# Seven-product sums in a transformer MLP: VectorE and ScalarE in written order while they run

## The chip, the cores and the metric

The kernel runs on one core of one Trainium2 chip. The metric is device time in microseconds (us) of one launch. Engines: TensorE (PE: matmuls, PEld: its weight loads), VectorE (DVE), ScalarE (ACT), GpSimd (POOL) and SyncE (SP, which issues the loads). SBUF is the working memory; PSUM holds matmul results in banks of 128 x 512 float32.

## The reference

Two residual layers over 256 positions and 2048 channels in float32. Each ends with a large MLP and a gated embedding; the token mixers ahead of the MLP are not touched by the change.

```python
for i in range(DEPTH):                      # DEPTH = 2
    ...                                     # token mixer, x = x + mixer(x) @ W_out
    h = rms_norm(x, mlp_norm[i])
    x = x + jnp.square(jax.nn.relu(h @ mlp_w1[i])) @ mlp_w2[i]     # 2048 -> 8192 -> 2048
    g = jax.nn.sigmoid(rms_norm(x, ple_norm[i]) @ ple_w_gate[i])
    x = x + g * (p[i] @ ple_w_proj[i])
return rms_norm(x, final_norm)
```

## The kernel before

Every float32 weight is used as two rounded halves, high and low, and every product as three matmuls (high-high, high-low, low-high). A weight tile of 128 x 2048 (1 MB) is loaded by SyncE into one of four raw buffers (`raw`, line 96). ScalarE writes its high half (L112), VectorE the low half as raw minus high (L117), both into one of four buffers `hl`. A matmul that reads the low half therefore waits for VectorE, one that reads only the high half for ScalarE. `Weights.run_ahead` (L129) issues splits up to three tiles ahead of the tile in use and loads two further ahead, unless `ws.hold` sets a lower limit on the splits.

The MLP of a layer runs over eight steps f = 0..7. A step for f < 7 is, in TensorE's order: block `w1(2f+2)` (first MLP matrix, four tiles, PSUM tiles `ps_h`), `w2(f,2)` and `w2(f,3)` (two column blocks of the second matrix, `ps_o`, two tiles each), then `pair(f)`, then block `w1(2f+3)`. Step 7 has no first block; it runs `w2(7,2)`, `pair(7)`, `pair_end`, `w2(7,3)`, and goes on to the embedding (`ps_e`, `ps_g`).

`pair(f)` makes the other two column blocks of the second matrix with seven products in place of eight, for two hidden blocks: fourteen products of six matmuls each, from seven `hl` tiles with two products in each. Numbered 0 to 13 in TensorE's order, the products of the second hidden block are 7 to 13; by their names p they are 1, 5, 2, 6, 3, 7, 4. Some weight operands are sums of raw tiles (VectorE, L109), so one tile here costs VectorE up to two additions and two half splits of 128 x 1024. The results stand in three PSUM pairs of banks, a (products 1 and 5), b (2 and 3), c (7 and 6), and a single bank d (4). `gather` takes them out when they are complete: a and c into `sums` (L657; for f = 0 by ScalarE, L655), b and d into x (L649, L651). There are three pairs of banks (`mm_pool`), so the two PSUM tiles of the next block `w1(2f+3)` take the pairs that a and b leave, and the block after it takes c first. `sm_pool` has two single banks: d and the transposes `tr_ple` share them.

Order: TensorE and SyncE keep the order of the code. For VectorE and ScalarE a list scheduler sets the order by priority, except inside `in_order()` (L255), where they too keep the order of the code; line 710 raises the priority of `pair_end` and line 751 on belongs to the embedding. `put_off` and `tick` delay a piece of code by so many steps; one product of the pair is a step, and so is one fourth of a tile elsewhere. `after.chunk(c, steps)` (L330) takes squares of a block of x on ScalarE and, `steps` later, transposes it on TensorE and writes it as `xT_ple` halves (L275, L280).

Of the kernel before, what the change touches and what calls it, by code (L numbers as in the profile page):

```python
# [29 lines left out]
PRIO = 400  # L30
# [119 lines left out]
def encoder(ctx: ExitStack, tc: tile.TileContext, a, out: bass.AP):  # L150
# [11 lines left out]
    ws = Weights(nc, raw_pool, hl_pool, 3, 2)  # L162
# [92 lines left out]
    def in_order():  # L255
        return tc.manual_schedule(engines={mybir.EngineType.Activation, mybir.EngineType.DVE})
# [5 lines left out]
    def tick():  # L262
        for entry in later[:]:
            entry[0] -= 1
            if entry[0] <= 0:
                later.remove(entry)
                entry[1]()
# [76 lines left out]
    def psum_mm(name):  # L344
        return mm_pool.tile([P, 1024], F32, tag="mm", name=name)
# [223 lines left out]
    def mlp(i, norm, after):  # L569
# [58 lines left out]
        def w2(f, n):  # L628
            ps = psum_mm(f"ps_o{i}_{f}_{n}")
            for q in (2 * f, 2 * f + 1):  # L630
                rows_product(ps, hidden[q], range(4), q == 2 * f, q == 2 * f + 1)
            add_to_x(ps, n)

        def pair(f):


            tiles = {}

            def psum(p):

                key, half = {1: ("a", 0), 5: ("a", 1), 2: ("b", 0), 3: ("b", 1), 7: ("c", 0), 6: ("c", 1), 4: ("d", 0)}[p]
                if key not in tiles:
                    name = f"ps_s{i}_{f}{key}"
                    tiles[key] = sm_pool.tile([P, 512], F32, tag="sm", name=name) if key == "d" else psum_mm(name)
                return tiles[key][:, half * 512:(half + 1) * 512]

            def gather(p):
                if p == 3:
                    nc.vector.tensor_tensor(x[:, 0, :1024], tiles["b"], x[:, 0, :1024], ALU.add)  # L649
                elif p == 4:  # L650
                    nc.vector.tensor_tensor(x[:, 1, :512], tiles["d"], x[:, 1, :512], ALU.add)  # L651
                elif p in (5, 7):
                    ps, to = (tiles["a"], sums[:, :1024]) if p == 5 else (tiles["c"], sums[:, 1024:])
                    if f == 0:
                        nc.scalar.activation(to, ps, AF.Copy)  # L655
                    else:
                        nc.vector.tensor_tensor(to, ps, to, ALU.add)  # L657

            k = 0
            for q in (2 * f, 2 * f + 1):  # L660
                h, g = hidden[q], forms[q]
                for p in SEVEN[q % 2]:
                    if k % 2 == 0:
                        w = ws.next()
                    for kt in range(2):
                        for m, (s, j) in enumerate(PASSES_W_MOVES):
                            act = {1: h[:, s, kt, :P], 2: h[:, s, 2 + kt, :P], 4: h[:, s, 2 + kt, P:], 5: g[:, s, 0, kt],
                                   6: g[:, s, 1, kt], 7: g[:, s, 2, kt], 3: g[:, s, 3, kt]}[p]
                            col = (k % 2) * 1024 + kt * 512
                            nc.tensor.matmul(psum(p), lhsT=act, rhs=w[:, j, col:col + 512],  # L670
                                             start=q % 2 == 0 and kt == 0 and m == 0,
                                             stop=q % 2 == 1 and kt == 1 and m == 2)
                    tick()
                    k += 1
                    if q % 2 and p in (6, 7, 4):
                        for done in {6: (5,), 7: (3,), 4: (7, 4)}[p]:
                            gather(done)

        def pair_end():
            m1, m5, m7, m6 = (sums[:, k * 512:(k + 1) * 512] for k in range(4))  # L680
            c11, c12, c21, c22 = (x[:, t, n * 512:(n + 1) * 512] for t in range(2) for n in range(2))
            add, sub = ((lambda to, p, q, op=op: nc.vector.tensor_tensor(to, p, q, op)) for op in (ALU.add, ALU.subtract))
            add(c11, c11, m1)
            sub(m6, m6, m1)
            sub(c21, c21, m6)
            add(c21, c21, m7)
            after.chunk(0, 10)
            sub(m5, m6, m5)
            add(c12, c12, m5)
            add(c22, c22, m5)  # L690
            sub(c22, c22, m7)
            after.chunk(1, 13)
# [5 lines left out]
        for f in range(8):  # L698
            if f < 7:
                w1(2 * f + 2)  # L700
            w2(f, 2)
            if f < 7:
                w2(f, 3)
                pair(f)
                w1(2 * f + 3)
                continue
            pT = embedding(i)
            after.chunk(2)
            pair(f)
            with tc.high_priority(offset=PRIO):  # L710
                pair_end()
            w2(f, 3)
            after.chunk(3, 8)
        return pT

    def embedding(i):
        pt = work.tile([P, 2, S], F32, name="pt", tag="sv")
        nc.sync.dma_start(out=pt, in_=a["pT"][i])
        pT = act_pool.tile([P, 2, 2, S], F32R, tag="act", name=f"pT{i}")
        divide_psum(halves(pT), pt, None)  # L720
        return pT
# [51 lines left out]

    nple = Norm("ple0", R_PLE)
    pT = mlp(0, norm, nple)
    norm = Norm("od", R_OD)
    order = ctx.enter_context(ExitStack())
# [70 lines left out]

    nple = Norm("ple1", R_PLE + 16)
    pT = mlp(1, norm, nple)  # L850
    gfin = act_pool.tile([P, D], F32, tag="act", name="gfin")
    nc.scalar.dma_start(out=gfin, in_=a["final_norm"].partition_broadcast(P))
# [110 lines left out]
```

## Time and profile before

| | |
|---|---|
| median of 3 runs | 2024.72 us (2023.49 to 2027.61) |
| profiled execution | 2022.2 us, span 2020.4 us |
| TensorE busy | 1947.5 us, 96% of the span |
| VectorE busy | 1564.6 us, 77% |
| ScalarE busy | 1043.6 us, 52% |
| granted TensorE clock, mean | 0.993 |
| HBM read | 373.75 MB, 186 GB/s over the span |

A row of the timeline gives the start in us from the span's start, the length, the engine, the line, what is written and read, and how many equal instructions follow each other; in brackets stands the idle time just before and what ended it. TensorE's matmuls overlap, so the length of a group is a little more than the distance to the next group's start. VectorE's instructions overlap by about 0.08 us in the same way.

### The profile page before, as it was taken

How to read it: one execution, taken by the hardware profiler on the slowest of the kernel's cores; microseconds unless marked ns; L12 is line 12 of the kernel's file. 1: busy time of each engine (PE TensorE's matmuls, PEld its weight loads, DVE VectorE, ACT ScalarE, POOL GpSimd, SP SyncE). 2: the span in 40 equal slices, each digit the busy share in tenths (PEclk: the TensorE clock that was granted, in tenths of full speed). 3: DMA queues.
4: the chain of work that ended last, by engine and by line, in shares of the span. 5: the costliest groups of instructions: out<-in, count | busy, mean ns of one | idle time of the engine just before them, and what ended most of it. 6: DMA issues, size and time to landing. Idle time of an engine off the chain costs nothing.

```text
span 2020.4 us, 24088 instructions
## 1 busy us (share of the span) xinstructions
PE 1947.5 (96%) x9730; PEld 1650.4 (82%) x9730; DVE 1564.6 (77%) x1771; ACT 1043.6 (52%) x1087; POOL 128.8 (6%) x65
## 2 busy tenths in 40 slices
PE   8999999999999999999999999999999999999897
PEld 6888888878787887877789888887887878787686
DVE  7988768796888869689656557977879687788854
ACT  6445555555455545545545445555545455455543
POOL 3875000000000000000001000000000000000000
PEclk9999999999999999999999999999999999999899
DMA  8545553645545464544443545545464554645532
GB/s 336 181 174 208 198 177 146 250 176 200 190 164 215 146 243 163 212 187 162 175 166 125 192 184 187 204 159 220 146 229 157 220 197 156 227 148 193 219 137 103
DMA packets 55664, 377.43 MB, mean 187 GB/s; under 512 B 6384, under 2 KB 6528, under 8 KB 11648
## 3 DMA queue, kind: packets, MB, share of 16 engines
q1 hardware_dynamic: 55152, 374.82, 50.6%
q8 instruction: 76, 1.25, 0.2%
q10 hardware_dynamic: 144, 1.05, 0.2%
q14 instruction: 36, 0.29, 0.0%
q0 software_dynamic: 256, 0.02, 0.0%
HBM read 373.75 MB, written 2.10 MB: 186 GB/s over the span
## 4 chain that ended last, share of the span: by engine, by line
PE 78%; DVE 17%; issue 3%; ACT 1%; DMA 1%; SPq 0%; ACTq 0%; DVEq 0%
PE ps_h L593 22%; PE ps_o L358 16%; PE ps_h L598 12%; DVE hl L117 10%; PE ps_g L358 8%; PE ps_od L358 4%; PE ps_in L358 4%; DVE raw L109 3%; PE ps_out L358 3%; PE ps_pool L358 2%; PE ps_outp L358 1%; PE ps_e L358 1%; DVE x L649 1%; DVE x L379 1%; PE ps_f L371 1%
## 5 line engine op out<-in xcount | busy, mean ns | idle before, releaser
L112 ACT ACTIVATE hl<-raw 128x2048 fp32r<-128x2048 f32 (+2 forms) x529 | 778.3, 1493 | 716.9 <-PE ps_h L598 281.1
L117 DVE TENSOR_TENSOR hl<-raw,hl 128x2048 fp32r<-128x2048 f32 (+3 forms) x501 | 863.2, 1745 | 325.4 <-ACT hl L112 324.0
L593 PE MATMUL ps_h<-xT_mlp,hl 128*128 128x512 f32 x2048 | 493.2, 392 | 28.6 <-DVE x L649 28.6
L593 PEld LDWEIGHTS ps_h<-xT_mlp,hl 128*128 128x128 f32 x2048 | 377.5, 189 | 106.8 <-issue 33.3
L358 PE MATMUL ps_o<-hl,h 128*128 128x512 f32 x1536 | 352.4, 390 | 0.0
L358 PEld LDWEIGHTS ps_o<-hl,h 128*128 128x128 f32 x1536 | 288.1, 188 | 59.3
L598 PEld LDWEIGHTS ps_h<-xT_mlp,hl 128*128 128x128 f32 x2048 | 262.8, 191 | 10.1
L598 PE MATMUL ps_h<-xT_mlp,hl 128*128 128x256 f32 x2048 | 266.1, 283 | 0.0
L358 PE MATMUL ps_g<-hl,xT_ple 128*128 128x512 f32 (+1 forms) x816 | 180.6, 382 | 0.0
L358 PEld LDWEIGHTS ps_g<-hl,xT_ple 128*128 128x128 f32 x816 | 148.1, 191 | 28.6 <-DVE hl L117 0.4
L117 POOL TENSOR_TENSOR hl<-raw,hl 128x2048 fp32r<-128x2048 f32 (+1 forms) x28 | 120.7, 4325 | 55.9 <-ACT hl L112 55.9
L358 PE MATMUL ps_in<-hl,xT_ev 128*128 128x512 f32 x384 | 90.8, 398 | 7.5 <-ACT hl L112 7.5
L455 DVE SCALAR_TENSOR_TENSOR acc<-vp,vT,acc 128x256 f32<-128x256 f32 x240 | 96.4, 485 | 0.1
L358 PEld LDWEIGHTS ps_in<-hl,xT_ev 128*128 128x128 f32 x384 | 73.3, 192 | 23.2 <-ACT hl L112 7.5
L608 ACT ACTIVATE relu<-ps_h 128x512 f32<-128x512 f32 x64 | 38.3, 598 | 97.4 <-PE ps_h L598 97.4
L358 PE MATMUL ps_od<-hl,f 128*128 128x512 f32 x384 | 88.1, 390 | 0.0
L358 PEld LDWEIGHTS ps_od<-hl,f 128*128 128x128 f32 x384 | 71.8, 188 | 14.7
L109 DVE TENSOR_TENSOR raw<-raw 128x1024 f32<-128x1024 f32 x64 | 78.1, 1220 | 0.6
L109 DVE TENSOR_TENSOR raw<-raw,raw 128x1024 f32<-128x1024 f32 x64 | 78.1, 1220 | 0.0
L609 DVE TENSOR_TENSOR relu<-ps_h,relu 128x512 f32<-128x512 f32 x64 | 43.8, 688 | 29.8 <-ACT relu L608 29.8
L812 POOL CAST top<-z 128x4 fp32r<-128x4 f32 x8 | 1.5, 188 | 907.8 <-DVE z L280 907.8
L624 ACT ACTIVATE g<-form 128x512 fp32r<-128x512 f32 x64 | 38.3, 624 | 22.6 <-DVE form L621 11.7
(283 smaller groups left out, 1695.7 us busy)
## 6 DMA issues: line engine op xcount, KB each, us to landing
raw<-in_mlp_w SPq DMA_DIRECT2D x256, 1024.0 KB, 4.9
raw<-in_ple_w_gate SPq DMA_DIRECT2D x32, 1024.0 KB, 4.9
raw<-in_w_in SPq DMA_DIRECT2D x20, 1024.0 KB, 4.8
raw<-in_ev_w_out SPq DMA_DIRECT2D x16, 1024.0 KB, 4.7
raw<-in_od_w_out SPq DMA_DIRECT2D x16, 1024.0 KB, 4.8
raw<-in_w_in SPq DMA_DIRECT2D x16, 256.0 KB, 6.1
raw<-in_ple_w_proj SPq DMA_DIRECT2D x8, 512.0 KB, 3.4
x<-in_x SPq DMA_DIRECT2D x2, 1024.0 KB, 7.8
```

The source lines that it names most:

```text
L109: self.nc.vector.tensor_tensor(src, src, self.raw[other[0]][:, other[1]:other[1] + w], ALU.add)
L112: self.nc.scalar.activation(hl[:, 0, to], src, AF.Copy)
L117: getattr(self.nc, lo).tensor_tensor(hl[:, 1, to], src, hl[:, 0, to].bitcast(F32), ALU.subtract)
L358: nc.tensor.matmul(ps[t][:, cols], lhsT=acts[:, s, kt, t * P:(t + 1) * P], rhs=w[:, m, kt * 512 + cols.start:kt * 512 + cols.stop], start= ...
L371: nc.tensor.matmul(out_ps, lhsT=w[sw], rhs=act[sa], start=bank_first and i == 0, stop=i == n - 1, skip_group_check=True)
L379: nc.vector.tensor_tensor(xs, ps[:, t * 512:(t + 1) * 512], xs, ALU.add)
L455: nc.vector.scalar_tensor_tensor(acc, src, cwT[:, ch, k:k + 1], acc, ALU.mult, ALU.add)
L593: nc.tensor.matmul(pss[p][:, e], lhsT=w[:, 0, ch], rhs=norm.xT[c][:, :, kt], start=c == 0 and kt == 0, stop=False, skip_group_check=True)
L598: nc.tensor.matmul(pss[p][:, e, 1], lhsT=w[:, 1, ch], rhs=norm.xT[c][:, 0, kt], start=False, stop=c == 3 and kt == 3, skip_group_check=True)
L608: nc.scalar.activation(r, pss[p][:, :, 1], AF.Copy)
L609: nc.vector.tensor_tensor(s, pss[p][:, :, 0], r, ALU.add)
L624: nc.scalar.activation(g[:, 0, to], src, AF.Copy)
```

## The change

Three things change. In `pair`, the splits of the tiles behind the pair's own seven are held back until product 3 of the second hidden block (number 11) has been issued; then `ws.hold` gets its old value. The evictions of a and b (`gather` 5 and 3) stand together behind product 3; those of c and d stand together at the end as before. And VectorE and ScalarE keep the order of the code in every pair, in the last one through `pair_end` too, whose raised priority goes. In the last step the transposes of the third block of x move from 4 steps behind the call to 16, which is behind the pair, into `w2(7,3)`.

```diff
@@ pair(f)
+            hold, ws.hold = ws.hold, min(ws.hold, ws.used + 7)
             k = 0
             for q in (2 * f, 2 * f + 1):
...
-                    if q % 2 and p in (6, 7, 4):
-                        for done in {6: (5,), 7: (3,), 4: (7, 4)}[p]:
+                    if q % 2 and p in (3, 4):
+                        for done in {3: (5, 3), 4: (7, 4)}[p]:
                             gather(done)
+                        ws.hold = hold
@@ mlp, steps 0 to 6
-                pair(f)
+                with in_order():
+                    pair(f)
                 w1(2 * f + 3)
@@ mlp, step 7
             pT = embedding(i)
-            after.chunk(2)
-            pair(f)
-            with tc.high_priority(offset=PRIO):
+            after.chunk(2, 16)
+            with in_order():
+                pair(f)
                 pair_end()
             w2(f, 3)
```

VectorE, step 1 of the first layer, from the last addition into raw79 on: hl84 and hl85 are the pair's last two tiles, hl86 to hl88 the first three of the next block, and ps_s0_1a, 1b, 1c, 1d the results a to d. Before:

```order
L117 TENSOR_TENSOR hl84_3445<-raw79_3370,hl84_3445 128x1024
L109 TENSOR_TENSOR raw78_3338<-raw78_3338,raw79_3370 128x1024
L117 TENSOR_TENSOR hl85_3467<-raw79_3370,hl85_3467 128x1024
L117 TENSOR_TENSOR hl84_3445<-raw78_3338,hl84_3445 128x1024
L657 TENSOR_TENSOR sums_119<-ps_s0_1a_3411,sums_119 128x1024
L109 TENSOR_TENSOR raw78_3338<-raw78_3338 128x1024
L117 TENSOR_TENSOR hl86_3488<-raw80_3443,hl86_3488 128x2048
L117 TENSOR_TENSOR hl85_3467<-raw78_3338,hl85_3467 128x1024
L117 TENSOR_TENSOR hl87_3505<-raw81_3465,hl87_3505 128x2048
L117 TENSOR_TENSOR hl88_3523<-raw82_3486,hl88_3523 128x2048
L649 TENSOR_TENSOR x_81<-ps_s0_1b_3418,x_81 128x1024
L657 TENSOR_TENSOR sums_119<-ps_s0_1c_3452,sums_119 128x1024
```

After, from the same place:

```order
L109 TENSOR_TENSOR raw78_3341<-raw78_3341,raw79_3373 128x1024
L117 TENSOR_TENSOR hl84_3450<-raw79_3373,hl84_3450 128x1024
L117 TENSOR_TENSOR hl84_3450<-raw78_3341,hl84_3450 128x1024
L109 TENSOR_TENSOR raw78_3341<-raw78_3341 128x1024
L117 TENSOR_TENSOR hl85_3472<-raw79_3373,hl85_3472 128x1024
L117 TENSOR_TENSOR hl85_3472<-raw78_3341,hl85_3472 128x1024
L657 TENSOR_TENSOR sums_119<-ps_s0_1a_3416,sums_119 128x1024
L649 TENSOR_TENSOR x_81<-ps_s0_1b_3423,x_81 128x1024
L117 TENSOR_TENSOR hl86_3521<-raw80_3448,hl86_3521 128x2048
L117 TENSOR_TENSOR hl87_3526<-raw81_3470,hl87_3526 128x2048
L117 TENSOR_TENSOR hl88_3529<-raw82_3491,hl88_3529 128x2048
L657 TENSOR_TENSOR sums_119<-ps_s0_1c_3457,sums_119 128x1024
```

The pair's own splits now come first, then the evictions of a and b, then the next block's three splits; before, the three splits stood ahead of the eviction of b, one of them ahead of the pair's last split.

VectorE at the end of step 7 of the first layer: hl193 is the pair's last tile, hl194 to hl196 are for `w2(7,3)` and `ps_e`, L682 and L685 are lines of `pair_end`. Before:

```order
L117 TENSOR_TENSOR hl193_6982<-raw168_6825,hl193_6982 128x1024
L657 TENSOR_TENSOR sums_119<-ps_s0_7a_6907,sums_119 128x1024
L117 TENSOR_TENSOR hl196_7038<-raw172_7001,hl196_7038 128x1024
L649 TENSOR_TENSOR x_81<-ps_s0_7b_6914,x_81 128x1024
L657 TENSOR_TENSOR sums_119<-ps_s0_7c_6967,sums_119 128x1024
L682 TENSOR_TENSOR x_81<-x_81,sums_119 128x512
L682 TENSOR_TENSOR sums_119<-sums_119 128x512
L651 TENSOR_TENSOR x_81<-ps_s0_7d_6988,x_81 128x512
```

After:

```order
L117 TENSOR_TENSOR hl193_6986<-raw168_6846,hl193_6986 128x1024
L657 TENSOR_TENSOR sums_119<-ps_s0_7a_6930,sums_119 128x1024
L649 TENSOR_TENSOR x_81<-ps_s0_7b_6937,x_81 128x1024
L117 TENSOR_TENSOR hl194_7035<-raw170_6962,hl194_7035 128x2048
L117 TENSOR_TENSOR hl195_7040<-raw171_6984,hl195_7040 128x2048
L117 TENSOR_TENSOR hl196_7043<-raw172_7005,hl196_7043 128x1024
L657 TENSOR_TENSOR sums_119<-ps_s0_7c_6971,sums_119 128x1024
L651 TENSOR_TENSOR x_81<-ps_s0_7d_6992,x_81 128x512
```

Here hl194 and hl195, which before stood ahead of hl193's last half, stand behind the evictions of a and b and ahead of those of c and d.

## Rows read from the trace of the kernel before

**Rows 1.** The page: span, and busy time of each engine.
```profile
span 2020.4 us, 24088 instructions
PE 1947.5 (96%) x9730; PEld 1650.4 (82%) x9730; DVE 1564.6 (77%) x1771; ACT 1043.6 (52%) x1087; POOL 128.8 (6%) x65
```
**Rows 2.** TensorE's waits: waiting and waited for, us in total, times, longest.
```profile
PE ps_h L593 <- DVE x L649: 28.6, 12, 2.4
PE ps_s_7d L670 <- DVE xT_ple L280: 7.7, 2, 4.4
...
PE ps_s_1d L670 <- DVE hl L117: 1.0, 2, 0.5
```
**Rows 3.** Timeline of TensorE, first layer, steps 0 and 1.
```profile
341.49 1.52 PE L670 MATMUL ps_s_0a<-hl,h 128*128 128x512 f32 x6
...
360.53 3.79 PE L593 MATMUL ps_h<-xT_mlp,hl 128*128 128x512 f32 x16
...
426.82 1.52 PE L670 MATMUL ps_s_1a<-hl,h 128*128 128x512 f32 x6
...
441.78 1.52 PE L670 MATMUL ps_s_1b<-hl,g 128*128 128x512 f32 x6
...
444.50 0.39 PE L670 MATMUL ps_s_1d<-hl,h 128*128 128x512 f32 x1
445.41 1.43 PE L670 MATMUL ps_s_1d<-hl,h 128*128 128x512 f32 x5 [0.51 <-DVE hl L117]
446.67 1.98 PE L593 MATMUL ps_h<-xT_mlp,hl 128*128 128x512 f32 x8
451.04 2.08 PE L593 MATMUL ps_h<-xT_mlp,hl 128*128 128x512 f32 x8 [2.39 <-DVE x L649]
```
**Rows 4.** Timeline of TensorE, first layer, start of the pair of step 2.
```profile
515.62 1.52 PE L670 MATMUL ps_s_2a<-hl,h 128*128 128x512 f32 x6
```
**Rows 5.** Timeline of VectorE, first layer, the pair of step 1.
```profile
427.02 1.29 DVE L379 TENSOR_TENSOR x<-ps_o,x 128x512 f32<-128x512 f32 x2 [0.44 <-PE ps_o L358]
...
430.50 1.22 DVE L109 TENSOR_TENSOR raw<-raw,raw 128x1024 f32<-128x1024 f32 x1
...
441.93 7.82 DVE L117 TENSOR_TENSOR hl<-raw,hl 128x2048 fp32r<-128x2048 f32 x4
...
449.67 1.22 DVE L649 TENSOR_TENSOR x<-ps_s_1b,x 128x1024 f32<-128x1024 f32 x1
450.81 1.22 DVE L657 TENSOR_TENSOR sums<-ps_s_1c,sums 128x1024 f32<-128x1024 f32 x1
```
**Rows 6.** Timeline of ScalarE, first layer, behind the pair of step 1.
```profile
449.14 1.91 ACT L112 ACTIVATE hl<-raw 128x2048 fp32r<-128x2048 f32 x1 [3.76 <-DMA raw<-in_mlp_w]
```
**Rows 7.** Groups by line and shape: count, busy us, mean ns, idle before.
```profile
L117 DVE TENSOR_TENSOR hl<-raw,hl 128x2048 fp32r<-128x2048 f32 x252 | 576.5, 2294 | 310.6 <-ACT hl L112 309.9
...
L117 DVE TENSOR_TENSOR hl<-raw,hl 128x1024 fp32r<-128x1024 f32 x232 | 277.5, 1220 | 9.4 <-ACT hl L112 8.6
...
L112 ACT ACTIVATE hl<-raw 128x1024 fp32r<-128x1024 f32 x236 | 243.3, 1057 | 216.8 <-DVE raw L109 90.3 <-PE ps_o L358 67.6 <-PE ps_g L358 12.2
```
**Rows 8.** The page's DMA issues: count, size, median us to landing.
```profile
raw<-in_mlp_w SPq DMA_DIRECT2D x256, 1024.0 KB, 4.9
```
**Rows 9.** Timeline of TensorE, step 7: first layer, then one row of the second.
```profile
926.42 1.52 PE L670 MATMUL ps_s_7a<-hl,h 128*128 128x512 f32 x6
...
952.79 11.92 PE L358 MATMUL ps_o<-hl,h 128*128 128x512 f32 x48
...
1878.52 2.90 PE L670 MATMUL ps_s_7d<-hl,h 128*128 128x512 f32 x6 [4.40 <-DVE xT_ple L280]
```
**Rows 10.** Timeline of VectorE, step 7: first layer, then one row of the second.
```profile
934.10 1.23 DVE L109 TENSOR_TENSOR raw<-raw,raw 128x1024 f32<-128x1024 f32 x1
...
964.98 1.29 DVE L379 TENSOR_TENSOR x<-ps_o,x 128x512 f32<-128x512 f32 x2
...
1885.00 1.23 DVE L657 TENSOR_TENSOR sums<-ps_s_7a,sums 128x1024 f32<-128x1024 f32 x1 [1.50 <-PE ps_s_7a L670]
```

## The prediction

> **What bounds the kernel now.** I read the page first. TensorE is busy 96% of 2020.4 us, VectorE 77%, ScalarE 52% [rows 1], so time can be won only where TensorE stands still, about 73 us in all. The table of TensorE's waits says where: 28.6 us in 12 waits of at most 2.4 us end with the eviction of b (L649), six lines like the one shown (steps 1 to 6, two layers each) give another 6 us for a low half that VectorE had not written, and 7.7 us in two waits belong to step 7 [rows 2]. Third, the timeline of steps 0 and 1. In step 0 the pair starts at 341.49 and the block behind it runs through from 360.53. In step 1 the last product is cut in two (444.50, then 445.41 after a wait for `hl`), and the block stops after eight matmuls until 451.04, for 2.39 us, on L649 [rows 3]. From pair start to pair start step 0 takes 426.82 - 341.49 = 85.33 us and step 1 takes 515.62 - 426.82 = 88.80 [rows 3, 4]. The same work, 3.47 us more.
>
> Fourth, VectorE in that pair. At its start VectorE waited for TensorE (0.44 us ahead of L379), so it is not behind; from 430.50 it runs without a gap, and its last four splits, from 441.93 on, end with the start of L649 at 449.67 [rows 5]. Product 11, which completes b, ended at 441.78 + 1.52 = 443.30 [rows 3]. So b lay complete for 6.4 us while splits for a later block were made. The bound in these 12 places is the order on VectorE.
>
> **The change, steps 1 to 6.** It adds and removes no instruction here, only places. I follow VectorE from the addition at 430.50, which stands first in both orders. Start to start, a split or addition of 1024 columns takes 1.14 us (1.22 less the overlap, as 449.67 to 450.81 shows) and a split of 2048 columns 2.20 (three of them and one of 1024 make 441.93 to 449.67) [rows 5, 7].
>
> - The pair's own rest is four additions and six half splits, ten times 1.14, so 430.50 + 11.4 = 441.9. Three of the half splits need a high half that ScalarE can begin only behind an addition, but another VectorE instruction of 1.14 lies between and ScalarE takes 1.06 [rows 7]; I add 0.2 and get 442.1.
> - Product 13 starts at 444.50 and needs this last split. It is there 2.4 us earlier, so the first wait goes: the block starts at 444.50 + 1.36 = 445.86 instead of 446.67 (1.36 is half the distance from 441.78 to 444.50, two products) [rows 3]. Gain 0.81. Product 10, at 441.78 - 1.36 = 440.42, needs the second half of hl84, two half splits and an addition before 442.1, so about 438.7: no new wait.
> - L657 takes a from 442.1 to 443.2. L649 then waits for product 11 until 443.30 and ends at 444.5. Behind it stand the splits hl86, hl87, hl88, then L657 of c and L651; the one who waits for those is TensorE, through the low halves. hl86 ends at 446.7, hl87 at 448.9, hl88 at 451.1.
> - The block needs a at 445.86 (there since 443.2), b eight matmuls later, near 447.7 (there since 444.5), and hl86's low half only after 16 matmuls, 3.6 us after its start, at 449.5 (there since 446.7). High halves come from ScalarE: behind hl85's last one at 440.9 it needs 1.91 for hl86, so 442.8 [rows 6]. hl87's low half is wanted after 32 large matmuls at the least, 3.8 us for 16 [rows 3], so beyond 453. Margins 2.6, 3.2, 2.8 and 4 us.
> - Loads. SyncE's order is unchanged. raw82 takes the buffer that hl85's first split frees, now 440.9; with 4.9 us for a load [rows 8] it lands at 445.8, ScalarE's half is there at 447.8 and VectorE's turn comes at 448.9. raw83 takes the buffer of hl85's last split, now 442.1. Before, ScalarE waited 3.76 us for such a load until 449.14 [rows 6]; it now has it earlier.
>
> So both waits go, 0.81 + 2.39 = 3.20 us by the waits, 3.47 by the periods. I take 3.4, in 12 pairs: 41 us. It costs VectorE nothing: c and d come out at 451 to 453 as before, and hl89 with them. What hides the later c is that its bank pair is wanted by the block after next only.
>
> VectorE's queue is served in order. In the second layer's step 7 L657 stood 1.50 us until product 8 had ended, with splits queued behind it [rows 10]. The Trainium skill, "PSUM — Partial Sum Buffer", section "Engine vs sequencer instructions", says the same as a rule: the queues of ScalarE and VectorE are strictly first in, first out. By that rule the new place of L649 is a risk that the old order did not have, since three splits stand behind an instruction that waits for TensorE. The arithmetic above holds that wait at 443.30 - 443.2, about 0.1 us.
>
> **The change, steps 0 and 7.** Step 0 had no wait [rows 3], and the eviction of b ahead of hl67 shifts nothing TensorE needs early: gain 0.
>
> Step 7 of the first layer runs from 926.42 to 952.79, where `w2(7,3)` starts [rows 9]. Fourteen products need 19.0 us, so 7.3 us are lost, 0.8 of them to the transposes, which now come later. The ceiling is thus 6.5 per layer, 13 in all. But VectorE comes late here: its addition at 934.10 is 7.7 us into the pair, against 430.50 - 426.82 = 3.7 in step 1 [rows 3, 5, 9, 10]. Without hl191's early half that addition moves to 933.0, and the pair's own splits end at 944.6. L657, L649 and hl194 then take 1.14 + 1.14 + 2.20, to 949.1. `w2(7,3)` could start at 946.3 and reads a low half with its second matmul, so it waits until about 949. Its third-block transposes then want the bank of d, which L651 frees near 954.3: another 2 us. And up to L379 of `ps_o_7_3` VectorE has 4 instructions of 1024, 4 of 2048, 9 of 512 (0.60 each, rows 10) and four quarter ones (estimate 0.4 from the shrinking of the larger ones): 4.6 + 8.8 + 5.4 + 1.6 = 20.4 us, 944.6 + 20.4 = 965.0, against 964.98 before [rows 10]. So in the first layer nothing is won. In the second VectorE's idle 1.50 us goes. There too six matmuls behind a wait of 4.40 us took 2.90 instead of 1.52 us [rows 9], a slowness that goes with the wait. I take 2 us for both layers, with bounds -4 (the two waits above come on top of the old ones) and +13.
>
> **Sum.** 41 + 2 = 43 us. The profiled execution took 2022.2 us, so 1979; the median of the runs, 2024.72, lies 2.5 above it, so 1982.
>
> **Rivals.**
> 1. *The wait moves to the low halves.* L649 holds hl86, and hl86 comes too late. Against it: 2.8 us of margin. For it: this margin stands on ten instructions that must follow without a gap, and VectorE's total is high, 1564.6 us [rows 1] in a program that would be 2% shorter. If half of the 3.4 us returns as waits for splits or loads, 20 us are won: 2004, between 1992 and 2018.
> 2. *Step 7 gives all it can.* VectorE's order would have to let `w2(7,3)` start as soon as the products end. Then 13 instead of 2: 1971.
> 3. *No change.* The held-back splits make the block wait for hl86 as long as it waited for b. It needs hl86 3.4 us later than worked out plus the margin of 2.8. 2020 to 2028.
> 4. *Slower, through c.* If the block's second PSUM tile takes the pair of banks that c leaves rather than b's, TensorE stands from 447.7 until L657 of c ends. With that at 452.2 (hl88 at 451.1 plus 1.14) each of 12 blocks waits 4.5 us where now 3.4 are lost, 13 us in all: 2038. It decides as soon as c's pair is the one taken. Against it: TensorE went on at 451.04, with the end of L649 (449.67 + 1.22) and ahead of the end of L657 of c (452.03) [rows 3, 5], and a and b are still released before c.
>
> **How the numbers follow.** Chances: forecast 0.64, rival 1 0.20, rival 2 0.06, rival 3 0.04, rival 4 0.06. The forecast's own range is 1976 to 1988 (3.2 to 3.6 us per pair, step 7 within -4 and +6, runs 2 us apart). Taking in step 7's full gain below and the larger part of rival 1 above gives 1972 to 2003. About 0.2%, 4 us, is what a measurement can tell from no change: faster 0.91 (forecast, rivals 1 and 2, with a hundredth to spare for the rest), same 0.03, slower 0.06.
>
> **What would show it.** In the profile after: no wait of `ps_h` on L649 and none of `ps_s_1d` to `ps_s_6d` on L117; L649 starting about 0.1 us behind product 11 and ending before its block begins; pair starts 85.3 us apart in all steps 0 to 5; L657 of c behind three full splits. Step 7: TensorE waits for hl194 at the start of `w2(7,3)` and for d's bank at the transposes, and L379 comes where it came before in the first layer. I am wrong if a wait for `hl` or for a load appears in the blocks behind the pairs (rival 1 or 3), or a wait on L657 (rival 4).

## The result, and the profile after

The changed kernel takes 1975.53 us in the median of four runs (1973.46 to 1977.62); the kernel before, run beside it, 2025.35 us (2023.49 to 2027.61). The ratio is 0.9754, with a 95% interval of 0.9737 to 0.977. The forecast was 1982. By the profiled executions, 2022.2 and 1976.2 us, 46.0 us were won where 43 were foretold. The median lies just below the forecast's own range, 1976 to 1988, and within the wider one, 1972 to 2003.

The page of the kernel after: span, then busy time, share of the span and instructions of each engine.

```profile
span 1974.4 us, 24094 instructions
PE 1937.8 (98%) x9730; PEld 1649.0 (84%) x9730; DVE 1567.8 (79%) x1771; ACT 1042.1 (53%) x1087; POOL 128.6 (7%) x65
```

The engines' counts of instructions are the same as before [rows 1]. Of the 46.0 us, TensorE's standing still gave 36.3 (72.9 us before, 36.6 after) and its busy time 9.7: cut by a wait, product 13 was busy for 0.39 + 1.43 us [rows 3] where it now takes 1.52, and some matmuls behind a wait were slower (below). TensorE's waits after (us in total, times, longest):

```profile
PE ps_o L358 <- DVE hl L117: 4.6, 2, 2.3
...
PE tr_ple L336 <- DVE x L651: 2.1, 2, 1.8
...
PE ps_s_7c L672 <- DVE hl L117: 1.5, 2, 0.8
```

The 28.6 us on L649 and the waits of `ps_s_1d` to `ps_s_6d` [rows 2] are gone. What is left on the MLP's side belongs to step 7: `ps_o` waits for hl194's low half, `tr_ple` for the bank that L651 frees, product 10 (`ps_s_7c`) for a low half. TensorE in steps 0 to 2 of the first layer, after:

```profile
343.12 1.52 PE L672 MATMUL ps_s_0a<-hl,h 128*128 128x512 f32 x6
...
428.45 1.52 PE L672 MATMUL ps_s_1a<-hl,h 128*128 128x512 f32 x6
...
443.41 1.52 PE L672 MATMUL ps_s_1b<-hl,g 128*128 128x512 f32 x6
...
446.13 1.52 PE L672 MATMUL ps_s_1d<-hl,h 128*128 128x512 f32 x6
447.49 3.79 PE L593 MATMUL ps_h<-xT_mlp,hl 128*128 128x512 f32 x16
...
513.78 1.52 PE L672 MATMUL ps_s_2a<-hl,h 128*128 128x512 f32 x6
```

Product 13 is no longer cut in two and the block's first 16 matmuls run in one piece, where they stood for 0.51 and 2.39 us [rows 3]. Pair start to pair start is 85.33 us in step 0 and 85.33 in step 1, against 85.33 and 88.80 before [rows 3, 4]. VectorE at the same place, after, with the three splits of the next block in the last row:

```profile
441.50 2.44 DVE L117 TENSOR_TENSOR hl<-raw,hl 128x1024 fp32r<-128x1024 f32 x2
443.86 1.22 DVE L657 TENSOR_TENSOR sums<-ps_s_1a,sums 128x1024 f32<-128x1024 f32 x1
444.99 1.21 DVE L649 TENSOR_TENSOR x<-ps_s_1b,x 128x1024 f32<-128x1024 f32 x1
446.12 6.68 DVE L117 TENSOR_TENSOR hl<-raw,hl 128x2048 fp32r<-128x2048 f32 x3
```

The pair's last split ends at 443.94 (441.50 + 2.44); TensorE wants it at 446.13. L649 starts 0.06 us behind the end of product 11 (443.41 + 1.52 = 444.93), so b is free at 446.20. The block wants it eight matmuls in, at 447.49 + 1.82 = 449.31 (16 of them take 3.63 to 3.65 from start to start). Slack 3.1 us, where before it was 2.4 us too late.

### The profile page after: what moved, and what is told of

It reads as the page before. It is cut to its first block, busy times and chain, and to the rows that moved or that the text cites. A ratio compares the mean times of both kernels' runs of the same rounds, so it can differ in the third digit from the quotient of the medians.

```text
span 1974.4 us, 24094 instructions
## 1 busy us (share of the span) xinstructions
PE 1937.8 (98%) x9730; PEld 1649.0 (84%) x9730; DVE 1567.8 (79%) x1771; ACT 1042.1 (53%) x1087; POOL 128.6 (7%) x65
## 3 DMA queue, kind: packets, MB, share of 16 engines
q8 instruction: 76, 1.25, 0.2%
## 4 chain that ended last, share of the span: by engine, by line
PE 92%; DVE 5%; issue 1%; ACT 1%; DMA 0%; SPq 0%; ACTq 0%
PE ps_h L593 23%; PE ps_o L358 16%; PE ps_h L598 12%; PE ps_g L358 8%; PE ps_od L358 4%; PE ps_in L358 4%; PE ps_out L358 3%; DVE hl L117 2%; PE ps_pool L358 2%; PE ps_e L358 1%; PE ps_outp L358 1%; DVE raw L109 1%; PE ps_f L371 1%; PE ps_z L802 1%; PE ps_s_6c L672 1%
## 5 line engine op out<-in xcount | busy, mean ns | idle before, releaser
L593 PE MATMUL ps_h<-xT_mlp,hl 128*128 128x512 f32 x2048 | 488.2, 390 | 0.0
L598 PEld LDWEIGHTS ps_h<-xT_mlp,hl 128*128 128x128 f32 x2048 | 262.6, 191 | 10.0
L598 PE MATMUL ps_h<-xT_mlp,hl 128*128 128x256 f32 x2048 | 266.0, 283 | 0.0
L624 ACT ACTIVATE g<-form 128x512 fp32r<-128x512 f32 x64 | 38.4, 624 | 22.6 <-DVE form L621 11.7
```

What stands on the lines that cost most here:

```text
L593: nc.tensor.matmul(pss[p][:, e], lhsT=w[:, 0, ch], rhs=norm.xT[c][:, :, kt], start=c == 0 and kt == 0, stop=False, skip_group_check=True)
L598: nc.tensor.matmul(pss[p][:, e, 1], lhsT=w[:, 1, ch], rhs=norm.xT[c][:, 0, kt], start=False, stop=c == 3 and kt == 3, skip_group_check=True)
L624: nc.scalar.activation(g[:, 0, to], src, AF.Copy)
```

## The experiments

Four questions. Does the gain sit in the places of the splits and evictions, or in the written order itself? Is the position of L649 against the three splits the cause, by dose? What is step 7 worth? Can step 7 be had better? The theory is that of the prediction: TensorE waited because splits for a later block stood ahead of the pair's own last split and of b's eviction. Its rivals: the freedom of the scheduler did the harm, wherever the splits stood; or the gain lies mostly in step 7.

| kernel | us, median | ratio to before | 95% interval |
|---|---|---|---|
| after | 1975.53 | 0.9754 | 0.9737 to 0.977 |
| step 7 as before | 1979.15 | 0.9782 | 0.9767 to 0.9796 |
| order only, steps 0 to 6 | 2034.78 | 1.0058 | 1.0043 to 1.0073 |
| hold and places, no order, steps 0 to 6 | 1985.77 | 0.9814 | 0.9799 to 0.9829 |
| one split ahead of b | 1975.07 | 0.9756 | 0.9742 to 0.9771 |
| two splits ahead | 1996.05 | 0.9858 | 0.9842 to 0.9874 |
| three splits ahead | 2055.94 | 1.0167 | 1.015 to 1.0184 |
| early transposes in step 7 | 1975.49 | 0.9763 | 0.9746 to 0.9781 |
| hl194 between a and b in step 7 | 1975.57 | 0.9759 | 0.9744 to 0.9773 |

**Step 7 as before.** The new order in steps 0 to 6 only.

```diff
-            hold, ws.hold = ws.hold, min(ws.hold, ws.used + 7)
+            hold, ws.hold = ws.hold, ws.hold if f == 7 else min(ws.hold, ws.used + 7)
...
+                    places = {6: (5,), 7: (3,), 4: (7, 4)} if f == 7 else {3: (5, 3), 4: (7, 4)}
...
-            after.chunk(2, 16)
-            with in_order():
-                pair(f)
+            after.chunk(2)
+            pair(f)
+            with tc.high_priority(offset=PRIO):
                 pair_end()
```

Expected: 

> Steps 0 to 6 as in the changed kernel, step 7 of both layers as in the kernel before (old gather places, no hold, scheduler's order, transposes 4 steps behind the call). Theory A (the wait for b's eviction in steps 1 to 6 is what the change took away, step 7 is a small extra): the twelve periods stay at 85.3 us, step 7 is as before, which by the two traces is 3.1 + 1.5 us longer; 4.6 us above the changed kernel, about 1980 (1977 to 1983). Rival B (the change lives from ScalarE and VectorE not being reordered at the end of each layer): 1995 or more.

Measured 1979.15 us, with all pair starts of steps 0 to 6 85.33 or 85.34 us apart, as in the changed kernel. By the two medians step 7 is worth 3.6 us. Taken against the kernel before that ran beside it (2023.31), this kernel gains 44.2 of the 49.8 us, which leaves 5.7; the spread of the runs cannot tell these two apart. The twelve pairs give the rest. The rival "step 7 gives most" is out.

**The written order alone.** Steps 0 to 6 keep `in_order()`, but no splits are held back and the evictions keep their old places.

```diff
-            hold, ws.hold = ws.hold, min(ws.hold, ws.used + 7)
+            hold, ws.hold = ws.hold, ws.hold if f < 7 else min(ws.hold, ws.used + 7)
...
+                    places = {6: (5,), 7: (3,), 4: (7, 4)} if f < 7 else {3: (5, 3), 4: (7, 4)}
-                    if q % 2 and p in (3, 4):
-                        for done in {3: (5, 3), 4: (7, 4)}[p]:
+                    if q % 2 and p in places:
+                        for done in places[p]:
```

Expected: 

> Steps 0 to 6 with the engines kept in code order, but without the hold and with the old gather places; step 7 as in the changed kernel. On VectorE hl86 and hl87 then stand ahead of a's eviction and hl88 ahead of b's. Theory A: no gain in steps 1 to 6: a out 2.0 us after the block wants it, b another 1.5 us late, 3.5 us per pair, as before; pair starts 88.8 apart; step 0 loses up to 3 us more; 1975.5 + 42 + 6 = 2023 (2015 to 2029). Rival C (order alone does it: the pair's own splits no longer mixed with others): 1975 to 1980.

Measured 2034.78 us: slower than before, and outside what was expected. TensorE's greatest waits in this kernel, then VectorE behind the pair of step 1, then TensorE behind the pairs of steps 1 and 2:

```profile
PE ps_h L593 <- DVE sums L657: 31.7, 12, 2.6
PE ps_h L593 <- DVE x L649: 7.7, 8, 1.3
```

```profile
446.01 4.49 DVE L117 TENSOR_TENSOR hl<-raw,hl 128x2048 fp32r<-128x2048 f32 x2 [0.58 <-ACT hl L112]
450.42 1.22 DVE L657 TENSOR_TENSOR sums<-ps_s_1a,sums 128x1024 f32<-128x1024 f32 x1
...
453.75 1.22 DVE L649 TENSOR_TENSOR x<-ps_s_1b,x 128x1024 f32<-128x1024 f32 x1
```

```profile
451.78 5.51 PE L593 MATMUL ps_h<-xT_mlp,hl 128*128 128x512 f32 x16 [2.63 <-DVE sums L657]
...
541.63 2.08 PE L593 MATMUL ps_h<-xT_mlp,hl 128*128 128x512 f32 x8 [2.64 <-DVE sums L657]
544.96 2.08 PE L593 MATMUL ps_h<-xT_mlp,hl 128*128 128x512 f32 x8 [1.25 <-DVE x L649]
```

The old code, in its own order, puts two of the next block's splits ahead even of a's eviction, and VectorE stands 0.58 us at the first of them, although a, whose eviction stands behind, was complete (product 8 ended at 442.34); the scheduler of the kernel before had put a's eviction ahead of all three. So TensorE now stands at the block's start, on a, for 2.63 us. In step 1 the 16 matmuls behind that take 5.51 us instead of 3.79. The granted clock there (columns: busy time and count of the five engines, PEclk, DMA share, GB/s):

```profile
451.80:456.00 4.20, 4.20 (x12) 3.08 (x13) 4.20 (x3) 1.91 (x1) 0.00 (x0) 0.59 1.01 423
```

A mean of 0.59 is mostly 1.2 GHz. In step 2, behind the same wait, the clock stays at 1.00, and TensorE then stands for b too, 1.25 us. Both cost about the same: from pair start to pair start it is 89.85 us in step 1 and 89.76 in step 2, 4.4 to 4.5 above 85.33. Expected were 2.0 us on a and 1.5 on b, 3.5 per pair. Twelve times the 0.9 more are 11 us, nearly all that the expectation was low; the fallen clock adds to it in some pairs only (92.00 us in step 3). What follows: the written order is no gain by itself, so the first rival falls.

**Hold and places without the order.** In steps 0 to 6 only `in_order()` is taken out.

```diff
-                with in_order():
-                    pair(f)
+                pair(f)
                 w1(2 * f + 3)
```

Expected: 

> Hold and new gather places kept, but in steps 0 to 6 VectorE and ScalarE are ordered by the scheduler; step 7 as in the changed kernel. hl86 then stands ahead of the pair's last split, and b's eviction behind that last split and ahead of hl87. Theory A: the wait of 2.4 us on L649 stays away, the wait of product 13 for the last split comes back (0.51 by the waits, 0.81 by the starts): periods of 86.1 us, 10 us above the changed kernel, about 1985 (1981 to 1989). Rival C (order alone): 2015 or more. Rival D (hold alone does all): 1975 to 1978.

Measured 1985.77 us, as expected. VectorE and TensorE in the pair of step 1:

```profile
443.23 1.22 DVE L657 TENSOR_TENSOR sums<-ps_s_1a,sums 128x1024 f32<-128x1024 f32 x1
...
445.49 3.42 DVE L117 TENSOR_TENSOR hl<-raw,hl 128x2048 fp32r<-128x2048 f32 x2
448.83 1.22 DVE L649 TENSOR_TENSOR x<-ps_s_1b,x 128x1024 f32<-128x1024 f32 x1
```

```profile
430.39 1.52 PE L672 MATMUL ps_s_1a<-hl,h 128*128 128x512 f32 x6
...
448.97 1.43 PE L672 MATMUL ps_s_1d<-hl,h 128*128 128x512 f32 x5 [0.51 <-DVE hl L117]
450.23 3.81 PE L593 MATMUL ps_h<-xT_mlp,hl 128*128 128x512 f32 x16
...
516.55 1.52 PE L672 MATMUL ps_s_2a<-hl,h 128*128 128x512 f32 x6
```

The scheduler still slips a's eviction and hl86 in ahead of the pair's last split (both kinds of split stand in the row of 3.42 us), so product 13 waits 0.51 us as before [rows 3], and the period is 86.16, 0.83 above 85.33. But b comes out at 450.05, before it is wanted at 450.23 + 1.82 = 452.05, and the long wait is gone. The two parts thus divide as the two waits do: the held splits and moved evictions take the 2.4 us wait, the written order the 0.8 (12 x 0.83 = 10.0; 1985.77 - 1975.53 = 10.2). The hold and the new places were not tried one without the other.

**Splits ahead of b, one, two and three.** The changed kernel, with n of the three held splits let through between the evictions of a and b in steps 0 to 6 (n = 1, 2, 3).

```diff
                         for done in {3: (5, 3), 4: (7, 4)}[p]:
+                            if done == 3 and f < 7:
+                                ws.hold = ws.used + 1 + n
+                                ws.run_ahead()
                             gather(done)
```

Expected, one split: 

> As e4_3_ahead, but only one split (hl86) stands ahead of b's eviction in steps 0 to 6. Theory A with its margin of 3 us: L649 ends 2.2 us later, about 0.9 us before the block's second tile wants b, so no wait and no change: 1975.5 (1973 to 1979). Rival E (any split ahead of the eviction costs its own time): 12 x 2.2 = 26 us more, 2002.

Expected, two: 

> Two splits (hl86, hl87) ahead of b's eviction in steps 0 to 6. Theory A: a wait of 1.3 to 1.5 us on L649 in 12 places, 16 to 18 us, and TensorE's granted clock stays at 1.00 behind it, as it did behind the 2.39 us of the kernel before: 1992 (1988 to 1996). Rival F (every wait at this place brings the clock down, as the 3.7 us in e4_3_ahead did, there for about 3 us a pair): 2020 to 2030. Rival E: 12 x 4.4 = 53, 2028.

Expected, three: 

> The changed kernel, but in steps 0 to 6 the hold is lifted between the two evictions, so that the next block's three splits hl86 to hl88 stand ahead of b's eviction; all else as in the changed kernel. Theory A: L649 ends 6.6 us later, 3.5 us after the block's second tile wants b: a wait of 3.5 us in 12 places, periods of 88.8, 1975.5 + 42 = 2017 (2013 to 2022); no wait of product 13. Rival C (the pair's own splits in sequence are the gain): 1975 to 1980.

Measured 1975.07, 1996.05 and 2055.94 us. VectorE's L649, first of the kernel with one split ahead, then with two, then with three (there in step 2):

```profile
445.48 1.22 DVE L649 TENSOR_TENSOR x<-ps_s_1b,x 128x1024 f32<-128x1024 f32 x1
```

```profile
451.61 1.22 DVE L649 TENSOR_TENSOR x<-ps_s_1b,x 128x1024 f32<-128x1024 f32 x1
```

```profile
541.89 1.22 DVE L649 TENSOR_TENSOR x<-ps_s_2b,x 128x1024 f32<-128x1024 f32 x1
```

TensorE with two splits ahead, and then with three:

```profile
430.67 1.52 PE L672 MATMUL ps_s_1a<-hl,h 128*128 128x512 f32 x6
...
449.71 1.98 PE L593 MATMUL ps_h<-xT_mlp,hl 128*128 128x512 f32 x8
452.88 2.11 PE L593 MATMUL ps_h<-xT_mlp,hl 128*128 128x512 f32 x8 [1.19 <-DVE x L649]
...
517.49 1.52 PE L672 MATMUL ps_s_2a<-hl,h 128*128 128x512 f32 x6
```

```profile
537.58 1.98 PE L593 MATMUL ps_h<-xT_mlp,hl 128*128 128x512 f32 x8
543.25 3.75 PE L593 MATMUL ps_h<-xT_mlp,hl 128*128 128x512 f32 x8 [3.70 <-DVE x L649]
546.80 2.81 PE L598 MATMUL ps_h<-xT_mlp,hl 128*128 128x256 f32 x16
```

The block starts 19.04 us behind the pair (449.71 - 430.67) and wants b 1.82 later. So b is early by 3.1 us in the changed kernel, by 0.9 with one split ahead (446.70 against 447.61, its pair starting at 426.75), and late by 1.3 with two (452.83 against 451.53) and by 3.7 with three (543.11 against 539.40): 2.2 to 2.4 us for each split, which is a split's length. From pair start to pair start it is 85.33, 85.34, 86.82 and, in step 2 with three splits, 610.21 - 518.54 = 91.67. With two splits the 1.49 us more, in 12 pairs, are 18; the time measured is 20.5 above the changed kernel. The other 3 us are in step 0, where TensorE waited too (430.67 - 343.77 = 86.90 us, 1.57 more, in two layers). With three the period there grows by 6.3 (5.5 to 7.1 over steps 1 to 5 of both layers), of which the wait is only 3.7. The rest stands in the two rows behind it: eight matmuls in 3.75 us where eight took 1.98, and 16 of L598 in 2.81 where they take 2.08 elsewhere. The clock in that stretch, with three splits and then with two:

```profile
543.25:549.45 6.20, 6.20 (x24) 5.43 (x25) 3.78 (x3) 0.00 (x0) 0.00 (x0) 0.58 0.95 390
```

```profile
452.88:456.74 3.86, 3.86 (x25) 3.52 (x25) 3.86 (x4) 1.92 (x1) 0.00 (x0) 1.00 0.98 384
```

The expectation of three splits was the wait alone, 2017; of the 39 us that it missed the slow matmuls make up some 30 (12 x 2.5), and step 0, 1.5 us longer per layer here too, 3. The place of L649 is shown to be the cause of the long wait, with its dose and with the point at which it begins.

In step 0 with two splits ahead, ScalarE and TensorE:

```profile
365.00 1.01 ACT L655 ACTIVATE sums<-ps_s_0c 128x1024 f32<-128x1024 f32 x1
```

```profile
366.06 2.11 PE L593 MATMUL ps_h<-xT_mlp,hl 128*128 128x512 f32 x8 [1.27 <-ACT sums L655]
```

TensorE goes on 0.05 us behind the eviction of c, while b's ended only at 366.38 (its L649 starts at 365.16). In step 0 ScalarE takes out c, and the block's second PSUM tile takes whichever of the two pairs of banks is released first: here c's. In the kernel before it was c's too: c was out at 361.33, b only at 364.55, and TensorE went through without a wait at 360.53 + 1.82 = 362.35. So in step 0 of that kernel the block does not take the pairs of a and b, as was said ahead of the prediction for every step. In the changed kernel b is out at 360.87 and c at 365.14, and TensorE goes through at 363.98: there it is b's.

**Early transposes in step 7.** The changed kernel with the third block's transposes at 4 steps again.

```diff
-            after.chunk(2, 16)
+            after.chunk(2)
```

Expected: 

> The changed kernel, with the third block's transposes in step 7 at 4 steps again instead of 16. Theory A: product 5 waits some 3 us per layer for the bank that a transpose holds, but VectorE, which is busy without a gap there, does the same work up to L379, so only little of it lasts: 1977 (1975 to 1981). Rival G (the place of the transposes is what step 7 gained): 1980 or more.

Measured 1975.49 us, no difference that can be told. TensorE's waits:

```profile
PE tr_ple L336 <- DVE rstd_ple L286: 6.6, 2, 3.3
...
PE ps_s_7d L672 <- DVE xT_ple L280: 5.1, 2, 2.5
```

The old wait of `ps_s_7d` (product 6) comes back (7.7 us before [rows 2], 5.1 here) and costs nothing that can be told. It takes the place of others: `w2(7,3)` then waits 1.33 us for hl194 where the changed kernel waits 2.30, no transposes wait for d's bank, and `ps_e` starts 36.57 us into the pair, 36.69 in the changed kernel. Behind it TensorE waits 3.3 us per layer at L286, for a chain over VectorE and ScalarE. That this chain sets the step's end is read from the trace and was not tested.

**hl194 between the evictions of a and b in step 7**, to start `w2(7,3)` earlier, with the third block's transposes at 20 steps.

```diff
                         for done in {3: (5, 3), 4: (7, 4)}[p]:
+                            if done == 3 and f == 7:
+                                ws.hold = ws.used + 2
+                                ws.run_ahead()
                             gather(done)
...
-            after.chunk(2, 16)
+            after.chunk(2, 20)
```

Expected: 

> The changed kernel, with two edits in step 7: hl194 is split between the evictions of a and b, and the third block's transposes come 20 steps behind the call, when d's bank is free. By the trace of the changed kernel this takes 1.1 us off the wait for hl194 and the wait on L651 (1.8 and 0.2 us). If TensorE's waits set the time there: 3 to 4 us won in all, 1972. If VectorE's work up to L379 sets it, as theory A has it: 0 to 2 us, 1974.5 (1971 to 1977).

Measured 1975.57 us, no gain. TensorE, the start of `w2(7,3)` and the wait behind it, first layer, then the second:

```profile
929.01 8.24 PE L358 MATMUL ps_o<-hl,h 128*128 128x512 f32 x35 [1.17 <-DVE hl L117]
...
1863.71 1.09 PE L336 MATMUL tr_ple<-ident,x 128*128 128x128 f32 x4 [4.15 <-DVE tot_ple L316]
```

`w2(7,3)` goes on after 1.17 us instead of 2.30, and the embedding's transposes then wait for VectorE, 1.95 us in the first layer and 4.15 in the second. No version is faster than the changed kernel beyond the spread of the runs.

## Why the prediction was right, and where a size was off

**Steps 1 to 6: right in mechanism and size.** Taken were 3.4 us per pair, 41 in all; the periods of the first layer give 88.80 - 85.33 = 3.47, twelve times 41.6 (one pair gave more, next paragraph). Step by step: VectorE's addition was to be followed without a gap, and the last split to end 15.3 us behind the pair's start (442.1 - 426.82). In the trace L657 of a starts 443.86 - 428.45 = 15.41 behind it. The wait of L649 for product 11, foretold as 0.1, did not come: VectorE reached it 0.06 us late. The rule that was weighed against the change, on queues that serve in order ("PSUM — Partial Sum Buffer", section "Engine vs sequencer instructions", in the Trainium skill), was not tested by this: the instruction at the head was ready. The order-only kernel agrees with it: there VectorE stood 0.58 us at a split, with the eviction of a, which was complete, behind it. The margin of 3.2 us for b came out at 3.1. No wait for a load or a low half appeared in the blocks behind the pairs, against rivals 1 and 3.

**The price of a wait: a little over its length in eleven pairs, more in one.** The forecast's 3.4 us lie between 3.20, the waits as it reckoned them, and 3.47, the first layer's period. From start to start the 2.39 us cost 2.66: the block's first 16 matmuls take 6.29 us in the kernel before (446.67 to the next row's start at 452.96) and 3.63 after. In the second layer's step 1 of the kernel before, the same wait had slow matmuls behind it:

```profile
1387.91 3.63 PE L593 MATMUL ps_h<-xT_mlp,hl 128*128 128x512 f32 x8 [2.38 <-DVE x L649]
```

Eight took 3.63 us where eight took 2.08 [rows 3], the granted clock was 0.53, and the period was 90.36. So the twelve pairs gave 11 x 3.47 + 5.03 = 43.2 us. The forecast read the first layer alone; that only one pair in twelve differed is luck, as a wait of 3.70 us with three splits ahead cost 6.3. And "time can be won only where TensorE stands still" was too narrow: 9.7 of the 46.0 us came out of its busy time.

**Step 0: right by the sum, for a reason not given.** The prediction found no wait there and did not say why b, evicted nearly as late as in step 1, held up nobody: in the kernel before the block had the banks of c there, which ScalarE took out early. Rival 4's mechanism, the block on c's banks, thus exists in step 0 of that kernel and of those with two and three splits ahead. In the changed kernel it did not occur: its blocks go on before c is out, in step 0 (363.98 against 365.14) as in step 1 (449.31 against 453.94).

**Step 7: the mis-sized term.** 2 us were taken. It is 3.6 by the run with the old step 7, whose trace gives the same (from the pair's start to the long stretch of `ps_g` 57.09 and 56.77 us in the two layers, 54.57 and 55.72 after). By the profiles before (57.67 and 57.18) and after it is 4.6. TensorE in step 7 of the first layer, and one row of the second:

```profile
907.30 1.52 PE L672 MATMUL ps_s_7a<-hl,h 128*128 128x512 f32 x6
...
930.25 2.80 PE L358 MATMUL ps_o<-hl,h 128*128 128x512 f32 x11 [2.30 <-DVE hl L117]
...
935.32 0.66 PE L336 MATMUL tr_ple<-ident,x 128*128 128x128 f32 x4 [1.84 <-DVE x L651]
...
1843.33 4.17 PE L358 MATMUL ps_o<-hl,h 128*128 128x512 f32 x11 [2.34 <-DVE hl L117]
```

The foretold waits are there: hl194 at the head of `w2(7,3)`, until 22.95 us into the pair (foretold 949 - 926.4 = 22.6), d's bank for 1.84. A third was not foretold: product 10 waits 0.76 us for a low half in each layer. And VectorE's L379:

```profile
945.97 1.27 DVE L379 TENSOR_TENSOR x<-ps_o,x 128x512 f32<-128x512 f32 x2
```

It comes 38.67 us into the pair, before 964.98 - 926.42 = 38.56 [rows 9, 10], as worked out. The step that failed is the one from there: "So in the first layer nothing is won". The work behind L379 does not hang on L379 alone. ScalarE, before and then after:

```profile
967.47 1.92 ACT L112 ACTIVATE hl<-raw 128x2048 fp32r<-128x2048 f32 x1 [0.19 <-PE ps_e L358]
```

```profile
946.91 1.92 ACT L112 ACTIVATE hl<-raw 128x2048 fp32r<-128x2048 f32 x1 [0.80 <-PE ps_e L358]
```

This split waits for the `hl` buffer that TensorE's `ps_e` frees, and the squares and transposed copies of the last block of x stand behind it on ScalarE. It starts 41.05 us into the pair before and 39.61 after: TensorE, past its waits sooner, frees the buffer 1.44 us earlier. That is about half of the first layer's 3.1; the rest lies behind it. Before, 18 matmuls of `ps_g` from 976.23 took 5.42 us; after they take 4.36. How much of this lasts is open: in the run with early transposes those 18 matmuls are slow again, 5.96 us, and the time is the same.

**Between the medians** the gain is 49.8, between the profiled executions 46.0. Before's median in this comparison is 3.2 above its profiled run, the changed kernel's 0.7 below. These are spreads of the runs, not further steps, and they make up some 3 of the 6.5 us between the forecast of 1982 and 1975.53; the other 3 are the 46.0 won against 43. The 46.0 add up within 0.2: 43.2 in the pairs and 4.6 in step 7, less 1.6 by which the untouched code ahead of the first pair ran longer in the profile after (343.12 against 341.49 us).

## What to carry to other kernels

When TensorE waits for PSUM banks, look at what stands ahead of the eviction in the evicting engine's queue: here work that was wanted later than the eviction was the cause, and each such instruction shifted the release by its own length. Work out the slack at the place (when the result is complete, when the bank is wanted) and let nothing longer than that in between; one split fitted here, two did not. A written order pays only with the right order written: the same `in_order()` with the old places was slower than the scheduler's.

## What the runs showed of the hardware that was not expected

A wait of TensorE can cost more than its length, and its length alone did not tell when. Each of four kernels has twelve like waits at the blocks behind the pairs of steps 1 to 6. The granted clock in the matmuls that followed left 1.00, which is 2.4 GHz, behind

- none of twelve waits of 1.19 to 1.20 us (two splits ahead);
- one of twelve of 2.35 to 2.39 us (kernel before);
- seven of twelve of 2.63 to 2.64 us (order only);
- all twelve of 3.63 to 4.45 us (three splits ahead).

Where it fell the figures above are means of 0.53 to 0.59, near 1.2 GHz. That cost 1.6 us in the one pair of the kernel before and 2.5 in a pair with three splits; in the order-only kernel the slow matmuls took the place of the wait for b, wholly or in part. In the changed kernel two nearly equal waits at the head of `w2(7,3)` went both ways. The clock behind 2.30 us in the first layer and behind 2.34 us in the second:

```profile
930.20:933.00 2.80, 2.75 (x13) 2.23 (x14) 2.80 (x2) 0.28 (x1) 0.00 (x0) 1.00 0.72 263
...
1843.30:1847.50 4.20, 4.17 (x13) 3.22 (x13) 4.20 (x3) 1.91 (x1) 0.00 (x0) 0.63 0.84 316
```

Ahead of both TensorE had run the same fourteen products with one short wait. Eleven matmuls took 2.80 us in the one and 4.17 in the other. And a wait of 3.26 us in product 6 of step 7 (`ps_s_7d`, first layer) left the clock at 1.00 in the kernel before, where six matmuls then took 1.62 us, and not in the kernel with the old step 7, where they took 2.90. What decides between them was not tried.
